# A transformer trunk's opening on one core: natural x tiles, two chunks transposed on TensorE, eight column tiles, modulation by VectorE row sums

## The chip, the cores and the metric

The kernel runs on one core of a Trainium2 chip. Its time is the device time of one launch in microseconds. A profile of one execution gives, for each engine (TensorE = PE, with its weight loads as PEld; VectorE = DVE; ScalarE = ACT; GpSimd = POOL; SyncE = SP, which issues most DMAs), every instruction with its start and its duration.

## The reference

Two inputs ("batches" 0 and 1), each 512 rows of 1024 columns, go through one layer with shared weights. What matters here is its beginning:

```python
def rms_norm(x, g):
    y = x * lax.rsqrt(jnp.mean(x * x, axis=-1, keepdims=True) + EPS)
    return y * g

c_act = jax.nn.silu(c)
mod = c_act @ w_ada + b_ada                       # (1024) @ (1024, 6*1024)
sh1, sc1, g1, sh2, sc2, g2 = split(mod, 6)
h = rms_norm(x, norm1_g) * (1.0 + sc1) + sh1
proj = h @ w_in                                   # (512, 1024) @ (1024, 2816)
q_a, k_a, v_a, q_r, k_r, v_r, g_r = split(proj, IN_OFFSETS, axis=-1)
...
x = x + g1 * (mix @ w_out)                        # mix: windowed attention and retention
h = rms_norm(x, norm2_g) * (1.0 + sc2) + sh2
x = x + g2 * (jnp.square(jax.nn.relu(h @ w_mlp1)) @ w_mlp2)
return rms_norm(x, final_g)
```

All is float32. A product is made of three matmuls of split operands: a high part (rounded to a shorter format, `fp32r`) and a low part (the rest); high × high, high × low, low × high.

## The kernel before

The work is staged in this order: an opening (batch 0's first norm, modulation and the first column tiles of its input projection), the mixer (the other projections of both batches, attention, retention, output projection), then the MLP for both batches together, and the last norm. Everything works on h transposed: 128 of the 1024 features on the partitions (a *chunk*, `kc` = 0 to 7), the 512 rows along the free axis.

The **opening** is written out by hand as a list of step names, `FRONT`; each name calls `step_<kind>(numbers)`, and the list's order is the order of each engine's instructions and of SP's DMA queue. Up to `P.7.0` this order is pinned. The steps that matter:

- `x.t` loads x. Before, this is a pair of chunks of x transposed on the host (`x0_t`, tile `xt`); `sq`, `ad` square them on ScalarE and add them on VectorE, `ns` sums over the partitions with a matmul against ones, `nc` and `nt` turn the sum into a column per row tile, `nv` adds epsilon, `nr` takes the power −0.5 on GpSimd.
- `rbt`, `rbc`: the factor of each row is spread over the partitions by four TensorE transposes (`row_factors`, tile `rb`) and copied; `xn`, `xh` multiply x by it on VectorE.
- `tr.kc.s` loads 128 columns of the modulation weights, transposed (s = 1 scale, 0 shift); `C.kc.s` multiplies them by the activated c, which `cbt`/`cbc` spread over all partitions (`cb`), and sums each row, one VectorE instruction of 1024 elements. Chunk 1 alone (`BOTH`) is summed for both batches by TensorE instead: `nat` loads, `pm` multiplies, `mr`, `pt`, `md` bring the result into columns.
- `wi.kc` loads the first `FIRST` columns of `w_in` for one chunk; `wh`, `wl` make their high and low parts.
- `hh`, `hm`, `hl` make the high part, the whole and the low part of h for one chunk from x, scale and shift.
- `P.kc.c`, `R.kc.c`, `Q.kc.c` are the three matmuls of chunk kc and column tile c into bank `first_c`. Eight PSUM banks exist.
- `warm.i.n` are n matmuls of zeros; `di`, `bias` make attention's distance table; `keep` stores the low parts for batch 1, and `rvl`, `rvh`, `rvs` start the next weights.

The **mixer** runs as *units* (`run_units`): one 128-column tile of a projection, with its weight load, split and 24 matmuls. Between halves of a unit, `between` looks up a digit in each of two strings: `SUMS` says how many background row sums (`background_mods`, one VectorE instruction of 1024 elements each, for all other modulation values) are issued there, `STAGES` how many steps of attention and retention. The first projection columns of batch 0 come out of the opening (`first`), all others are units. For batch 1 the high parts are made anew and the low parts are loaded back.

Of the kernel before, what the change touches and what calls it, by code (L numbers as in the profile page):

```python
# [15 lines left out]
P = 128  # L16
# [12 lines left out]
FIRST = 896  # L29
BOTH = (1,)  # L30
# [3 lines left out]
def trunk_kernel(ctx, tc, x0, x1, x0_t, x1_t, params, gate2_bias, w_ada_first, w_ada_t, w_ada_gate2, w_in_first, w_in,  # L34
# [143 lines left out]
    xt0 = {}  # L178
# [27 lines left out]
    gm = const.tile([P, NB, KC], F32, name="gm")  # L206

    def background_mods():


        todo = [(s, kc, (1,)) for kc in range(KC) if kc not in BOTH for s in (1, 0)]
# [6 lines left out]
        for n, (sec, kc, bs) in enumerate(todo):  # L218
            t, nxt = nxt, load(n + 1)
# [346 lines left out]
    def tick_stage(force=False):  # L566
# [4 lines left out]
        for a in active:  # L571
            if a[1] <= clock[0] or force:
# [60 lines left out]

    unit_of = {c: i for i, c in enumerate([*range(FIRST, 1792, P), *range(2304, 2816, P)])}

    def proj_unit(hT, col, name, done):
        key = f"in{col}"

        def load():
            if hT is hT_of[1]:  # L640
# [95 lines left out]
    def out_units(b, late=None):  # L736
# [46 lines left out]
        def unit(hf, kq):  # L783
# [4 lines left out]
            def load():  # L788
# [6 lines left out]
                if kq == 2:  # L795
                    gr[hf] = gate_row(0, b, hs)
# [207 lines left out]
    wi, raws, halves, sums, mr, hm, banks, open_banks = {}, {}, {}, {}, {}, {}, {}, {}  # L1004
    order = (4, 5, 0, 1, 2, 3, 6)
    kept_first = tc.dram_tile((P, KC, FIRST), F32, name="kept_first")
    for c in range(FIRST // P):
        kept_lows[f"in{c * P}"] = kept_first[:, :, c * P:(c + 1) * P]
# [52 lines left out]
    def step_ns(n):

        if n == 0:
            banks["ns"] = aux_bank("ns")
        src = one["sq", 0][:, 0, :] if n == 2 else one["sq", 3][:, n, :]
        nc.tensor.matmul(banks["ns"][:2, :], ones, src, start=n == 0, stop=n == 2)

    def step_nc():
        one["ns"] = f2("ns")
        nc.scalar.copy(one["ns"][:2, :], banks["ns"][:2, :])  # L1070

    def step_nt():
        for t in range(NT):
            nc.tensor.transpose(banks["ns"][:, 2 * t:2 * t + 2], one["ns"][:2, t * P:(t + 1) * P], ident[:2, :2])

    def step_nv():
        one["v"] = small([P, NT], "nv")
        nc.vector.tensor_scalar(one["v"], banks["ns"][:, 0:2 * NT].rearrange("p (t o) -> p t o", o=2)[:, :, 0], 1.0 / D, EPS,
                                ALU.mult, ALU.add)

    def step_nr():
        one["r"] = small([P, NT], "nr")
        nc.gpsimd.tensor_tensor(one["r"], one["v"], neghalf[:, :NT], ALU.pow)
# [11 lines left out]
    def step_xh(k):  # L1095
        nc.vector.tensor_tensor(xt0[0][:, k, :], xt0[0][:, k, :], banks["rb"], ALU.mult)

    def step_pm(kc, q):

        if q == 0:  # L1100
            sums[kc] = aux_bank(f"pm_{kc}")
        w = halves[kc, q // 2].rearrange("p (k n) -> p k n", n=256)
        for k in range(2 * q, 2 * q + 2):
            nc.tensor.matmul(sums[kc][:NB, :256], cact[:, k, :], w[:, k % 4, :], start=k == 0, stop=k == KC - 1,
                             skip_group_check=True)

    def step_mr(kc):
        mr[kc] = mwork.tile([NB, 256], F32, tag="st", name=f"mr_{kc}", bufs=8)
        nc.scalar.copy(mr[kc], sums[kc][:NB, :256])

    def step_pt(kc):
        for c in range(2):
            nc.tensor.transpose(sums[kc][:, 256 + c * 2:258 + c * 2], mr[kc][:, c * P:(c + 1) * P], ident[:NB, :NB])

    def step_md(kc):
        m = [sums[kc][:, 256 + c * 2:258 + c * 2] for c in range(2)]
        nc.vector.tensor_scalar(mod_a[0][:, kc, :], m[1], onep[:, kc:kc + 1], gcol[0][:, kc:kc + 1], ALU.add, ALU.mult)
        nc.vector.tensor_scalar(mod_s[0][:, kc, :], m[0], bcol[:, kc:kc + 1], None, ALU.add)
# [9 lines left out]
    def step_wh(kc):  # L1128
        w = [r4(f"wi{s}_{kc}").rearrange("p a n -> p (a n)")[:, :FIRST] for s in "hl"]
        nc.scalar.copy(w[0], wi[kc][:, :FIRST])  # L1130
        raws[kc], wi[kc] = wi[kc], w

    def step_wl(kc):
        w = wi[kc]
        nc.vector.tensor_sub(w[1], raws.pop(kc)[:, :FIRST], f(w[0]))
# [12 lines left out]
    def step_P(kc, c):  # L1148
        if kc == 0:
            open_banks[c] = (mm_bank if c < 3 else aux_bank)(f"first_{c}")  # L1150
        w, h_, cs = wi[kc], hm[kc][0], slice(order[c] * P, (order[c] + 1) * P)
        nc.tensor.matmul(open_banks[c], w[0][:, cs], h_[:, 0, :], start=kc == 0, stop=False)

    def step_R(kc, c):
        w, h_, cs = wi[kc], hm[kc][0], slice(order[c] * P, (order[c] + 1) * P)
        nc.tensor.matmul(open_banks[c], w[1][:, cs], h_[:, 0, :], start=False, stop=False)
# [23 lines left out]
    def step_rvs(kq):  # L1180
# [4 lines left out]
    steps = dict(rvl=step_rvl, rvh=step_rvh, rvs=step_rvs, x=step_x, nat=step_nat, tr=step_tr, wi=step_wi, tanh=step_tanh, cact=step_cact, cbt=step_cbt, cbc=step_cbc,  # L1185
                 sq=step_sq, ad=step_ad, ns=step_ns, nv=step_nv, nr=step_nr, rbt=step_rbt, rbc=step_rbc, xn=step_xn,
                 pm=step_pm, mr=step_mr, pt=step_pt, nc=step_nc, nt=step_nt, md=step_md, C=step_C, wh=step_wh, wl=step_wl, hm=step_hm, hh=step_hh,
                 hl=step_hl, P=step_P, R=step_R, Q=step_Q, xh=step_xh, keep=step_keep, warm=step_warm, di=masked_distance,
                 bias=bias_table)
    FRONT = """  # L1190
x.0 warm.0.11 x.1 x.2 di.0 di.1 x.3 di.2 bias.0 bias.1 tr.0.1 bias.2 bias.3 tanh sq.0 cact tr.0.0
cbt.0 bias.4 cbt.1 cbc.0 sq.1 warm.1.7 nat.1.0 bias.5 ad.1 sq.2 wi.0 cbt.2 cbt.3 cbc.1 sq.3.0
warm.2.2 ad.2 sq.3.1 ns.0 nat.1.1 bias.6 bias.7 ns.1 ad.3 wi.1 C.0.1 ns.2 warm.3.3 tr.2.1 nc cbc.2
nt pm.1.0 tr.2.0 nv cbc.3 nr wh.0 C.0.0 warm.4.2 wi.2 rbt pm.1.1 xh.0 pm.1.2 tr.3.1 wl.0 hh.0 hm.0
P.0.0 P.0.1 tr.3.0 P.0.2 rbc P.0.3 hl.0 P.0.4 P.0.5 xh.1 P.0.6 pm.1.3 wi.3 C.2.1 R.0.0 mr.1 R.0.1
wh.1 R.0.2 tr.4.1 R.0.3 pt.1 R.0.4 md.1 R.0.5 wl.1 R.0.6 hh.1 Q.0.0 tr.4.0 Q.0.1 Q.0.2 hm.1 Q.0.3
xn.1 Q.0.4 Q.0.5 wh.2 Q.0.6 wi.4 P.1.0 P.1.1 hl.1 P.1.2 P.1.3 C.2.0 P.1.4 P.1.5 tr.5.1 P.1.6 R.1.0
R.1.1 wh.3 R.1.2 C.3.1 R.1.3 R.1.4 tr.5.0 hh.2 R.1.5 R.1.6 Q.1.0 hm.2 Q.1.1 C.3.0 Q.1.2 Q.1.3 Q.1.4
Q.1.5 Q.1.6 P.2.0 wl.2 wi.5 P.2.1 hh.3 P.2.2 tr.6.1 P.2.3 P.2.4 hm.3 hl.2 P.2.5 P.2.6 R.2.0 wh.4
xn.2 R.2.1 tr.6.0 R.2.2 R.2.3 R.2.4 R.2.5 C.4.1 R.2.6 Q.2.0 Q.2.1 Q.2.2 Q.2.3 Q.2.4 C.4.0 Q.2.5  # L1200
Q.2.6 P.3.0 P.3.1 wh.5 P.3.2 P.3.3 wl.3 wi.6 tr.7.1 P.3.4 P.3.5 tr.7.0 hh.4 P.3.6 hl.3 hm.4 R.3.0
R.3.1 R.3.2 C.5.1 R.3.3 R.3.4 R.3.5 R.3.6 Q.3.0 Q.3.1 C.5.0 Q.3.2 Q.3.3 wh.6 Q.3.4 Q.3.5 Q.3.6 P.4.0
# [445 lines left out]
```

## Time and profile before

| What | Value |
|---|---|
| median of 3 runs | 1091.72 us (1091.71 to 1092.14) |
| the profiled execution | 1093.01 us, of which the span of its instructions is 1091.2 us |
| TensorE / VectorE / ScalarE / GpSimd busy in the span | 99% / 79% / 49% / 4% |
| mean DMA rate over the span | 204 GB/s |
| opening, to the last matmul into `first` | 58.3 us |

A row of the timeline reads: start, duration, engine, line, operation, output tile, inputs, shapes, count; in brackets how long the engine was idle before it, and what ended that. A duration includes the engine's start-up, which overlaps the instruction before, so what one instruction costs in a full stream is the distance from start to start. A row of waits reads: who waited for whom, us in total, times, longest.

### The profile page before, as it was taken

The numbers are of one execution on the slowest core, as the hardware profiler recorded it, in microseconds if no ns is written. First come the engines' busy times: TensorE is split into PE (matmuls) and PEld (weight loads), VectorE is DVE, ScalarE is ACT, GpSimd is POOL, SyncE is SP. The second block draws the span as 40 slices with busy tenths as digits, with TensorE's granted clock in tenths as the row PEclk, the third lists the DMA queues.
The fourth block names the chain that finished last, engine by engine and source line by source line (L and its number), as shares of the span: only waits on it lengthen the run. The fifth ranks groups of instructions, "written<-read, shape, count | busy, mean of one in ns | idle before, by whom it ended". The sixth has DMA issues, their size and how long they took to land.

```text
span 1091.2 us, 14043 instructions
## 1 busy us (share of the span) xinstructions
PE 1077.9 (99%) x5018; PEld 886.1 (81%) x5018; DVE 866.8 (79%) x1456; ACT 536.9 (49%) x907; POOL 48.6 (4%) x55
## 2 busy tenths in 40 slices
PE   9999999999999999999999999999999999999997
PEld 4878887778888888898788888888888888888886
DVE  7979988887878885999787787866569754589786
ACT  6477768547754442574333333433353633334342
POOL 0000000000000001010000000000000000003213
PEclk9999999999999999999999999999999999999999
DMA  9776877665556889535554455543973556525504
GB/s 368 262 265 208 285 267 250 209 226 177 186 178 209 290 305 355 178 115 191 180 173 169 145 193 174 184 145 108 327 298 114 180 192 215 186 78 193 193 20 155
DMA packets 85083, 222.24 MB, mean 204 GB/s; under 512 B 8195, under 2 KB 22547, under 8 KB 85013
## 3 DMA queue, kind: packets, MB, share of 16 engines
q1 hardware_dynamic: 84420, 220.76, 58.5%
q8 instruction: 39, 0.64, 0.2%
q10 hardware_dynamic: 432, 0.57, 0.2%
q14 instruction: 32, 0.25, 0.1%
q0 software_dynamic: 160, 0.02, 0.0%
HBM read 161.80 MB, written 59.52 MB: 203 GB/s over the span
## 4 chain that ended last, share of the span: by engine, by line
PE 51%; DVE 0%; POOLq 0%; issue 0%; ACT 0%; POOL 0%; ACTq 0%
PE x L1418 16%; PE px_None L967 13%; PE y L1418 12%; PE py_None L967 10%; PE pg L266 0%; PE pg L265 0%; DVE x2r L1487 0%; POOLq L1644 0%; DVE x2r L1460 0%; DVE acc L1459 0%; ACT jkf L1466 0%; POOL msf L1469 0%; ACTq L1466 0%
## 5 line engine op out<-in xcount | busy, mean ns | idle before, releaser
L1358 DVE TENSOR_TENSOR uc_l<-ur,uc_h 128x1024 fp32r<-128x1024 f32 x56 | 68.3, 1221 | 52.3 <-ACT uc_h L1358 35.1
L1418 PE MATMUL x<-wc_l,uc_h 128*128 128x512 f32 (+1 forms) x264 | 101.0, 383 | 0.0
L1418 PE MATMUL x<-wc_h,uc_l 128*128 128x512 f32 (+1 forms) x264 | 101.0, 383 | 0.0
L1418 PE MATMUL x<-wc_h,uc_h 128*128 128x512 f32 (+1 forms) x264 | 100.8, 383 | 0.0
L1358 ACT CAST uc_h<-ur 128x1024 fp32r<-128x1024 f32 x56 | 58.8, 1050 | 77.2 <-PE x L1418 25.1
L1418 PE MATMUL y<-wc_h,uc_h 128*128 128x512 f32 x192 | 74.7, 389 | 0.0
L1418 PE MATMUL y<-wc_l,uc_h 128*128 128x512 f32 x192 | 74.7, 389 | 0.0
L1418 PE MATMUL y<-wc_h,uc_l 128*128 128x512 f32 x192 | 74.7, 389 | 0.0
L1358 ACT CAST wc_h<-w 128x1024 fp32r<-128x1024 f32 x48 | 50.5, 1051 | 48.1 <-PE x L1418 24.7
L1358 DVE TENSOR_TENSOR wc_l<-w,wc_h 128x1024 fp32r<-128x1024 f32 x48 | 58.5, 1220 | 17.6 <-ACT wc_h L1358 13.8
L1418 PEld LDWEIGHTS x<-wc_h,uc_l 128*128 128x128 f32 x264 | 49.6, 188 | 9.7
L1418 PEld LDWEIGHTS x<-wc_h,uc_h 128*128 128x128 f32 x264 | 49.6, 188 | 9.7
L1418 PEld LDWEIGHTS x<-wc_l,uc_h 128*128 128x128 f32 x264 | 49.6, 188 | 9.6
L152 PE MATMUL po<-wh_wo,ms 128*128 128x512 f32 x128 | 50.4, 394 | 0.0
L153 PE MATMUL po<-wh_wo,ms 128*128 128x512 f32 x128 | 50.0, 390 | 0.0
L199 DVE CUSTOM_DVE_ANT_0 jka_b<-raw_adat,cb,cols 128x1024 bf16<-128x1024 f32 x39 | 49.0, 1280 | 0.1
L872 ACT CAST wc_s4h<-raw_w 128x1024 fp32r<-128x1024 f32 x16 | 16.9, 1054 | 63.7 <-PE px_None L967 49.5
L1418 PEld LDWEIGHTS y<-wc_h,uc_l 128*128 128x128 f32 x192 | 36.0, 188 | 7.5
L1418 PEld LDWEIGHTS y<-wc_h,uc_h 128*128 128x128 f32 x192 | 36.0, 188 | 7.4
L1418 PEld LDWEIGHTS y<-wc_l,uc_h 128*128 128x128 f32 x192 | 36.0, 188 | 7.4
L391 ACT ACTIVATE st<-st,negm 128x256 f32<-128x256 f32 (+1 forms) x64 | 35.2, 555 | 9.5 <-DVE negm L386 9.5
L967 PE MATMUL py_None<-hch,wc_a 128*128 128x512 f32 x120 | 39.6, 389 | 0.0
(393 smaller groups left out, 2957.6 us busy)
## 6 DMA issues: line engine op xcount, KB each, us to landing
ur<-spill SPq DMA_DIRECT2D x56, 512.0 KB, 4.5
raw_adat<-in_w_ada_t_dram SPq DMA_DIRECT2D x38, 512.0 KB, 5.4
raw_w<-in_w_mlp_dram SPq DMA_DIRECT2D x32, 512.0 KB, 3.6
spill<-s SPq DMA_DIRECT2D x64, 256.0 KB, 3.6
w<-in_w_mlp_dram SPq DMA_DIRECT2D x32, 512.0 KB, 4.7
spill<-u SPq DMA_DIRECT2D x48, 256.0 KB, 2.0
raw_ada<-in_w_ada_t_dram SPq DMA_DIRECT2D x14, 512.0 KB, 9.8
x<-in_x_dram SPq DMA_DIRECT2D x12, 512.0 KB, 7.3
```

The source lines that it names most:

```text
L152: nc.tensor.matmul(ps, lhs[0], rhs[0], start=start and not low_first, stop=False)
L153: nc.tensor.matmul(ps, lhs[late], rhs[1 - late], start=False, stop=stop and low_first)
L199: nc.vector.tensor_tensor_reduce(junk(f"jka_{name}_{sec}_{kc}_{b}"), t, cb[:, b, :], 1.0, bcol[:, sec * KC + kc:sec * KC + kc + 1] if bias ...
L391: nc.scalar.activation(st[hh][:, :w], st[hh][:, :w], AF.Exp, bias=negm[:, hh:hh + 1], scale=0.125, accum_out=den[:, hh:hh + 1])
L872: nc.scalar.copy(hi, src)
L967: self.last = nc.tensor.matmul(bank[:, cs], x[:, k, :], y, start=first and k == 0 and i == 0, stop=last and k == 3 and i == 2, skip_group_ ...
L1358: last_split[:] = [nc.scalar.copy(hi, src), nc.vector.tensor_sub(lo, src, f(hi))]
L1418: nc.tensor.matmul(out, left[n][x][:, i, ts_], right[n][y][:, i, cs], start=first and i == 0 and k == 0, stop=end and i == 1 and k == 2, s ...
```

## The change

The opening loads x for the norm in natural layout (128 rows of 1024), squares and sums each tile in one ScalarE instruction, and makes the factor per tile on GpSimd. The first 256 columns of x are scaled per row and transposed by TensorE, which gives chunks 0 and 1; chunks 2 to 7 still come from host-transposed pairs (`xp`). Chunk 1's modulation is made by row sums as all others, chunk 0's by halves of 512 (`Ch`), loaded in halves (`trh`). The opening makes eight column tiles instead of seven (the first retention key tile is the new one), and the projection columns are gathered on the host in the order in which they are used. Two guards, `made_through`, see to it that a background value is made before its reader is written. `SUMS`, `STAGES` and `FRONT` are new; of these a line each is shown.

```diff
-FIRST = 896
-BOTH = (1,)
+FIRST = (512, 640, 0, 128, 256, 384, 768, 1280)
+UNITS = tuple(c for c in (*range(768, 1792, P), *range(2304, 2816, P)) if c not in FIRST)
...
-        todo = [(s, kc, (1,)) for kc in range(KC) if kc not in BOTH for s in (1, 0)]
+        todo = [(s, kc, (1,)) for kc in range(KC) for s in (1, 0)]
...
-    SUMS = ("100100012110011201001001100022000002222100210020110002021021"
+    SUMS = ("110100021002200210100011000010021201221010002110100202120001"
...
+                    made_through(2, KC - 1)
                     gr[hf] = gate_row(0, b, hs)
...
     def step_x(t):
-        xt0[t] = load_x_pair(0, t)
+        xn0[t] = load_x_tile(0, t)
+
+    def step_xp(t):
+        xt0[t] = load_x_pair(0, t)
...
-    def step_nat(kc, kh):
-        t = halves[kc, kh] = r4f(f"raw_ada1_{kc}_{kh}")
-        in_order(nc.sync.dma_start(t, w_ada_first[BOTH.index(kc), kh]))
+    def step_trh(s, hf):
+        if hf == 0:
+            halves[0, s] = r4f(f"raw_ada1_0_{s}")
+        cs = slice(hf * 512, (hf + 1) * 512)
+        in_order(nc.sync.dma_start(halves[0, s][:, cs], w_ada_t[s, 0][:, cs]))
...
-    def step_sq(t, kc=None):
-        if not kc:
-            one["sq", t] = r4(f"sq_{t}", F32)
-        part = slice(0, 2) if kc is None else slice(kc, kc + 1)
-        nc.scalar.activation(one["sq", t][:, part, :], xt0[t][:, part, :], AF.Square)
-    def step_ad(t): ...
-    def step_ns(n): ...
-    def step_nc(): ...
-    def step_nt(): ...
+    def step_sq(t):
+        one["ss", t] = small([P, 1], f"ss_{t}")
+        nc.scalar.activation(junk(f"jkx_{t}"), xn0[t], AF.Square, scale=D ** -0.5, accum_out=one["ss", t])
+
+    def step_nv(t):
+        one["v", t] = small([P, 1], f"nv_{t}")
+        nc.gpsimd.tensor_scalar(one["v", t], one["ss", t], EPS, None, ALU.add)
+
+    def step_nr(t):
+        if t == 0:
+            one["r"] = small([P, NT], "nr")
+        nc.gpsimd.tensor_tensor(one["r"][:, t:t + 1], one["v", t], neghalf[:, 0:1], ALU.pow)
+
+    def step_xs(t):
+        part, r = xn0[t][:, :2 * P], one["r"][:, t:t + 1]
+        if t > 1:
+            nc.scalar.activation(part, part, AF.Copy, scale=r)
+        else:
+            nc.vector.tensor_scalar(part, part, r, None, ALU.mult)
...
+    def step_xt(t):
+        for c in range(2):
+            if t == 0:
+                banks["x", c] = (aux_bank, mm_bank)[c](f"pxc_{c}")
+            nc.tensor.transpose(banks["x", c][:, t * P:(t + 1) * P], xn0[t][:, c * P:(c + 1) * P], ident)
+
+    def step_xc():
+        one["x1"] = f2("xc1")
+        nc.scalar.copy(one["x1"], banks["x", 1])
+
+    def x_chunk(kc):
+        return banks["x", 0] if kc == 0 else one["x1"] if kc == 1 else xt0[kc // 2][:, kc % 2, :]
...
-    def step_pm(kc, q): ...
-    def step_mr(kc): ...
-    def step_pt(kc): ...
-    def step_md(kc): ...
+    def step_Ch(s, hf):
+        cs, a_ = slice(hf * 512, (hf + 1) * 512), (mod_s, mod_a)[s][0][:, 0, 0:1]
+        if hf == 0:
+            one["C", s] = small([P, 1], f"cs_{s}")
+        nc.vector.tensor_tensor_reduce(junk(f"jka_h_{s}_{hf}")[:, :512], halves[0, s][:, cs], cb[:, 0, cs], 1.0,
+                                       one["C", s] if hf else onep[:, 0:1] if s else bcol[:, 0:1], ALU.mult, ALU.add,
+                                       a_ if hf else one["C", s])
+        if hf and s:
+            nc.vector.tensor_tensor(a_, a_, gcol[0][:, 0:1], ALU.mult)
...
-    def step_wh(kc):
-        w = [r4(f"wi{s}_{kc}").rearrange("p a n -> p (a n)")[:, :FIRST] for s in "hl"]
-        nc.scalar.copy(w[0], wi[kc][:, :FIRST])
-        raws[kc], wi[kc] = wi[kc], w
+    def step_wh(kc, hf=None):
+        if not hf:
+            raws[kc], wi[kc] = wi[kc], [r4(f"wi{s}_{kc}").rearrange("p a n -> p (a n)") for s in "hl"]
+        cs = slice(0, 1024) if hf is None else slice(hf * 512, (hf + 1) * 512)
+        (nc.scalar.copy if hf is None else nc.vector.tensor_copy)(wi[kc][0][:, cs], raws[kc][:, cs])
...
     FRONT = """
...
+Ch.1.1 wi.1 nr.3 xt.2 warm.4.3 xs.3 Ch.0.0 xt.3 xp.1 rbt Ch.0.1 xc warm.5.5 wh.0.0 tr.2.1 hh.0
...
-    first = attn_units(hT_of[0], 0) + head_0[:1]
+    first = attn_units(hT_of[0], 0) + head_0[:2]
...
+    def made_through(sec, kc):
+        while background and made[-1:] in ([], [(sec, kc)]) or (sec, kc) not in made:
+            tick_background()
...
+            made_through(0, kc)
             h_high(1, kc, src, dst)
...
-    run_units(units, 1.3, {5: lambda: extra.append(norm_x1())}, 0.6)
+    run_units(units, 1.3, {4: lambda: extra.append(norm_x1())}, 0.6)
```

More of the change, by code (lines that the diff above doesn't have):

```diff
@@ L218, in background_mods @@
         for n, (sec, kc, bs) in enumerate(todo):
+            made.append((sec, kc))
             t, nxt = nxt, load(n + 1)
@@ L632, in run_units @@
                 hooks[n]()
-    unit_of = {c: i for i, c in enumerate([*range(FIRST, 1792, P), *range(2304, 2816, P)])}
+    unit_of = {c: i for i, c in enumerate(UNITS)}
     def proj_unit(hT, col, name, done):
@@ L1001, in store @@
                 nc.sync.dma_start(spill[g][p, :, i, :], t)
[L1004 to L1008, printed above, removed]
+    wi, raws, halves, hm, banks, open_banks = {}, {}, {}, {}, {}, {}
+    kept_first = tc.dram_tile((P, KC, 1024), F32, name="kept_first")
+    for c, col in enumerate(FIRST):
+        kept_lows[f"in{col}"] = kept_first[:, :, c * P:(c + 1) * P]
     def step_x(t):
+        xn0[t] = load_x_tile(0, t)
+    def step_xp(t):
         xt0[t] = load_x_pair(0, t)
-    def step_nat(kc, kh):
-        t = halves[kc, kh] = r4f(f"raw_ada1_{kc}_{kh}")
-        in_order(nc.sync.dma_start(t, w_ada_first[BOTH.index(kc), kh]))
+    def step_trh(s, hf):
[3 more added lines that the diff above has]
+        in_order(nc.sync.dma_start(halves[0, s][:, cs], w_ada_t[s, 0][:, cs]))
     def step_tr(kc, s):
@@ L1061, in step_ns @@
[L1061 to L1074, printed above, removed]
@@ L1093, in step_xn @@
         x_scale(xt0[t], one["rb"])
[L1095 to L1118, printed above, removed]
+    def step_Ch(s, hf):
[7 more added lines that the diff above has]
+            nc.vector.tensor_tensor(a_, a_, gcol[0][:, 0:1], ALU.mult)
     def step_C(kc, s):
@@ L1183, in step_rvs @@
         first_v[kq].loaded([x.rearrange("p (a n) -> p a n", n=512) for x in w])
[L1185 to L1189, printed above, removed]
@@ L1190, in trunk_kernel @@
-    FRONT = """
[L1191 to L1195, printed above, removed]
@@ new lines, in trunk_kernel @@
+    FRONT = """
+x.0 x.1 warm.0.11 di.0 x.2 di.1 di.2 x.3 bias.0 trh.1.0 bias.1 bias.2 trh.1.1 bias.3 trh.0.0 tanh
+sq.0 cact trh.0.1 cbt.0 cbt.1 nv.0 cbc.0 sq.1 warm.1.4 wi.0 nr.0 cbc.1 cbt.2 xs.0 nv.1 sq.2 tr.1.1
+nr.1 cbt.3 cbc.2 warm.2.3 xs.1 nv.2 sq.3 cbc.3 xt.0 tr.1.0 nr.2 xt.1 warm.3.6 Ch.1.0 xs.2 nv.3
+Ch.1.1 wi.1 nr.3 xt.2 warm.4.3 xs.3 Ch.0.0 xt.3 xp.1 rbt Ch.0.1 xc warm.5.5 wh.0.0 tr.2.1 hh.0
+wh.0.1 hm.0 P.0.0 wl.0 P.0.1 tr.2.0 P.0.2 rbc P.0.3 P.0.4 bias.4 P.0.5 hl.0 P.0.6 bias.5 P.0.7 wi.2
@@ L1604, in _laid_out @@
                             + [np.tile(a[n].reshape(1, -1), (P, 1)) for n in ('ret_decay_fwd', 'ret_decay_bwd', 'attn_sink')], 1)
-    units = np.concatenate([w_in[:, FIRST:1792], w_in[:, 2304:2816]], 1)
+    columns = lambda cols_: np.concatenate([w_in[:, c:c + P] for c in cols_], 1)
     out = dict(
```

80 lines of the change are left out of this document (38 added, 42 removed).

## The prediction

> **What bounds the kernel now.** I read the page's busy shares first, then the span cut at the first projection matmul and at the end of the opening, then TensorE's waits and its timeline.
>
> ```profile
> PE 1077.9 (99%) x5018; PEld 886.1 (81%) x5018; DVE 866.8 (79%) x1456; ACT 536.9 (49%) x907; POOL 48.6 (4%) x55
> 0.00:17.66 17.66, 15.41 (x67) 6.20 (x67) 13.06 (x26) 11.29 (x19) 2.56 (x8) 1.00 0.91 347
> 17.66:58.30 40.64, 40.29 (x175) 31.82 (x175) 34.30 (x55) 21.91 (x31) 0.00 (x0) 1.00 0.82 310
> 58.30:250.00 191.70, 189.30 (x912) 154.71 (x911) 170.92 (x404) 130.43 (x261) 5.05 (x5) 1.00 0.70 239
> 17.66 1.66 PE L1152 MATMUL first<-h,wih 128*128 128x512 f32 x6
> 19.66 0.47 PE L1152 MATMUL first<-h,wih 128*128 128x512 f32 x1 [0.35 <-DVE xt L1096]
> 20.07 1.02 PE L1104 MATMUL pm<-raw_ada,cact 128*2 128x256 f32 x4
> 29.52 1.75 PE L1152 MATMUL first<-h,wih 128*128 128x512 f32 x7
> 31.11 1.75 PE L1156 MATMUL first<-h,wil 128*128 128x512 f32 x7
> 58.31 0.39 PE L152 MATMUL pj_rv<-wh_rv,h 128*128 128x512 f32 x1
> ```
>
> A row of stretches reads: length, then busy time of PE, PEld, DVE, ACT, POOL, granted clock, DMA share, GB/s. TensorE is busy 99% of the span, so outside the opening a saving is worth something only if it takes TensorE work away or lets that work begin earlier. In the first 17.66 us TensorE is busy too, but with `warm` matmuls and small sums: no product of the reference's projections is made before `P.0.0` at 17.66. From there it never stops for long, so the end of the kernel is, to first order, the start of `P.0.0` plus the TensorE work behind it plus the few waits. Seven matmuls go by in 31.11 − 29.52 = 1.59 us, 0.227 each; seven column tiles of three products and eight chunks are 168 of them, 38.1 us, while the opening takes 58.31 − 17.66 = 40.65. The 2.5 over are 0.35 of waiting, 1.0 for the four `pm` matmuls inside the stream, and some 1.1 of slow first matmuls, small transposes and slips.
>
> **The start of `P.0.0`.** In the old opening the last wait before it is a chain through the sum of squares, the transposed factor and the scaled x. In the new one the chain is: last x tile lands, ScalarE squares it with a row sum, GpSimd adds epsilon and takes the power, ScalarE scales 256 columns, TensorE transposes, then the rows of the factor and five `warm` matmuls that stand ahead of `P.0.0` on TensorE.
>
> On GpSimd, between the identity matrix and the first norm of batch 1, stood one power over four columns:
>
> ```order
> L487 IOTA dl 128x896
> masks.py:199 AFFINE_SELECT ident<-ident 128x128
> L1083 TENSOR_TENSOR nr<-nv,neghalf 128x4
> L1244 TENSOR_TENSOR r_x_1566<-v_x_1281,neghalf 128x4
> L470 TENSOR_TENSOR rrs_0_1904<-rva_0_1902,neghalf 128x4
> ```
>
> Now, at the same place (`nv` is the mean square plus epsilon, `nr` its power −0.5):
>
> ```order
> masks.py:199 AFFINE_SELECT ident<-ident 128x128
> L1062 TENSOR_SCALAR nv_160<-ss_142 128x1
> L1067 TENSOR_TENSOR nr<-nv_160,neghalf 128x1
> L1062 TENSOR_SCALAR nv_181<-ss_163 128x1
> L1067 TENSOR_TENSOR nr<-nv_181,neghalf 128x1
> L1062 TENSOR_SCALAR nv_199<-ss_183 128x1
> L1067 TENSOR_TENSOR nr<-nv_199,neghalf 128x1
> L1062 TENSOR_SCALAR nv_224<-ss_201 128x1
> L1067 TENSOR_TENSOR nr<-nv_224,neghalf 128x1
> ```
>
> Epsilon moved from VectorE to GpSimd, and four pairs in a row stand ahead of everything that x feeds. On ScalarE the squares and the first chunk stood so:
>
> ```order
> L1052 ACTIVATE sq_172<-xt_2_123 128x1024
> L1052 ACTIVATE sq_187<-xt_3_128 128x512 x2
> L505 ACTIVATE bias_t<-di 128x384 x2
> L1070 COPY ns<-ns 2x512
> L1130 CAST wih_229<-raw_wi_174 128x896
> L308 ACTIVATE h_0_0_251<-xt_0_105,mod_s_89,mod_a_87 128x512
> ```
>
> and now (`x` is a natural tile, `pxc`/`xc` the two transposed chunks):
>
> ```order
> L1058 ACTIVATE jkx_184,ss_183<-x_2_125 128x1024
> L1058 ACTIVATE jkx_202,ss_201<-x_3_129 128x1024
> L1072 ACTIVATE x_2_125<-x_2_125,nr 128x256
> L1072 ACTIVATE x_3_129<-x_3_129,nr 128x256
> L1084 COPY xc_252<-pxc_207 128x512
> L310 ACTIVATE h_0_0_264<-pxc_205,mod_s_89,mod_a_87 128x512
> ```
>
> The weight cast has left ScalarE's queue (VectorE does it), bias tables moved behind `h`, and two scalings that wait for GpSimd stand ahead of `h`.
>
> ```profile
> 0.73 1.83 SPq L175 DMA_DIRECT2D xt<-in_x_t_dram  x4
> DMA to landing us min/median/max: 4.5/6.1/6.9
> GB/s 0 116 357 419 423 415 407 406 410 406 414 401 413 412 407 412 409 393 419 126 8 271 393 325 76 367 382 244 256 0 19 197 358 409 421 429 397 419 390 416
> 14.03 0.94 ACT L1130 CAST wih<-raw_wi 128x896 fp32r<-128x896 f32 x1 [0.70 <-DMA raw_wi<-in_w_in_first_dram]
> L294 ACT ACTIVATE jk<-x 128x1024 bf16<-128x1024 f32 x4 | 4.2, 1062 | 0.0
> L399 ACT ACTIVATE st<-st,rden 128x256 f32<-128x256 f32 x8 | 3.6, 500 | 0.7 <-DVE rden L396 0.7
> 16.67 0.81 ACT L308 ACTIVATE h<-xt,mod_s,mod_a 128x512 fp32r<-128x512 f32 x1 [1.70 <-DVE xt L1096]
> 7.08 1.67 PE L1172 MATMUL warm<-idle 128*128 128x512 bf16 x7
> 15.26 0.65 PE L301 MATMUL rb<-ident,nr 128*128 128x128 f32 x4
> 1062.41 0.27 POOL L1469 TENSOR_SCALAR msf<-ssf,msf 128x1 f32<-128x1 f32 x1 [13.15 <-ACT jkf L1466]
> 1065.96 2.11 POOL L1473 TENSOR_TENSOR rf<-msf,neghalf 128x1 f32<-128x1 f32 x4
> 1043.92 0.80 POOL L1469 TENSOR_SCALAR msf<-ssf 128x1 f32<-128x1 f32 x1 [0.34 <-ACT jkf L1466]
> 1043.45 1.22 DVE L1358 TENSOR_TENSOR wc_l<-w,wc_h 128x1024 fp32r<-128x1024 f32 x1
> ```
>
> The first x tile lands at 0.73 + 4.5 = 5.2; behind it the queue moves some 410 GB/s, 1.28 us for 512 KB. (Check: old `wi.0` is six such loads and one of 448 KB later, 5.2 + 7.7 + 1.1 = 14.0, where the cast that waited for it starts.) So x.3 lands at 9.05. Its square takes 1.06 and about 0.1 for reading the sum: 10.25. GpSimd: 0.27 for epsilon and 0.54 for the power, 11.1. Beside it VectorE runs row sums with two SBUF operands; the 0.80 row, which ended 0.05 after the VectorE subtraction beside it, shows that such an operation can hold GpSimd. For this the bounds are 0 and one 512-wide row sum (half of 1.28) for each of the two, 1.3; I take 0.5, nearer to the lower end, since VectorE waits for the landing of a half between these row sums and lets go there: 11.65. Scaling 256 columns 0.50, two transposes 0.3 (quarters of the 0.65), rows of the factor 0.65, five `warm` (`warm.5.5` in the new table) at 0.24: 14.3; six hand-offs at about 0.05 make it **14.6** (13.9 without the GpSimd hold and with shorter hand-offs; 15.5 with both holds whole). The branch over `xc` (0.6) and `h` (0.81) is shorter, 14.0. The modulation is no later: four halves of 256 KB land by 9.05 + 2.56 = 11.6, and the last row sum ends near 13.3; `wi.0` lands at 12.9 and its first half is cast by 13.7.
>
> So `P.0.0` comes 17.66 − 14.6 = 3.1 us earlier.
>
> **The opening's length.** Eight columns are 192 matmuls, 43.6 us. The wait of 0.35 and the 1.0 of `pm` are gone, and its small transposes with it; of the slips I keep 1.0. VectorE has to keep pace:
>
> ```profile
> 36.36 1.28 DVE L199 CUSTOM_DVE_ANT_0 jka_f<-raw_ada,cb,onep 128x1024 bf16<-128x1024 f32 x1
> 37.76 1.28 DVE L199 CUSTOM_DVE_ANT_0 jka_f<-raw_ada,cb,cols 128x1024 bf16<-128x1024 f32 x1
> 38.97 1.08 DVE L1135 TENSOR_TENSOR wil<-raw_wi,wih 128x896 fp32r<-128x896 f32 x1
> 39.97 0.68 DVE L314 TENSOR_TENSOR h<-hm,h 128x512 fp32r<-128x512 f32 x1
> 40.57 1.22 DVE L305 TENSOR_TENSOR xt<-xt,rb 128x1024 f32<-128x1024 f32 x1
> ```
>
> By starts, a chunk costs it 1.40 + 1.21 for the two row sums, 1.00 × 1024/896 = 1.14 for the low halves, 0.60 for `hl` and half of 1.14 for `xn`: 4.9 us against 24 × 0.227 = 5.45 on TensorE. Chunk 1, formerly summed on TensorE, now costs VectorE 2.6 here: after `hl.0` (about 16.0) its two sums end near 18.7, `h` of chunk 1 near 19.5, due at 14.6 + 5.45 = 20.05. It fits by half a microsecond and the slack grows by 0.5 a chunk. The loads grow from 27 to 31 times 512 KB (x a second time for three pairs, weights of 512 instead of 448 KB); at 1.28 each the last could land at 43.6, wanted near 47. Hidden, with 3 us to spare. ScalarE was busy 21.9 of 40.6 and takes four bias rows more; hidden. End: 14.6 + 43.6 + 1.0 = 59.2, 0.9 later than before, with one column tile more done.
>
> **Behind the opening.** One projection unit is gone: 24 × 0.227 = 5.45 us of TensorE. Against this VectorE gets two more 1024-wide row sums in the background (chunk 1 of batch 1) and loses one weight split, and has 5.45 us less time for the rest.
>
> ```profile
> L199 DVE CUSTOM_DVE_ANT_0 jka_b<-raw_adat,cb,cols 128x1024 bf16<-128x1024 f32 x39 | 49.0, 1280 | 0.1
> L102 DVE TENSOR_TENSOR wl_rk<-raw_rk,wh_rk 128x1024 fp32r<-128x1024 f32 x4 | 4.9, 1220 | 0.0
> PE psc L381 <- DVE mx L383: 0.6, 1, 0.6
> PE pj_rq L148 <- DVE wl_rq L102: 0.5, 1, 0.5
> PE pyb L480 <- ACT ryn L475: 0.4, 1, 0.4
> PE pj_rv L152 <- DVE qs L359: 0.3, 1, 0.3
> PE pvt_a L344 <- ACT vt_a L338: 0.3, 1, 0.3
> PE pj_rv L152 <- DVE ks L332: 0.2, 1, 0.2
> ```
>
> From 58.3 to 250 VectorE is idle 191.70 − 170.92 = 20.8 us and TensorE waits 2.3 in all (the six rows). With +2.6 − 1.2 of work and 5.45 less time the idle is 13.9; in proportion the waits become 2.3 × 20.8/13.9 = 3.4. I take +1.0. The bounds are −1 (new tables that leave half of today's waits) and +4 (VectorE's extra work plus half of the lost 5.45 shows). `made_through` issues no wait of its own; it can only bunch row sums, which this bound covers. The hook moved from unit 5 to 4 is the same unit. Longer `keep` stores and one more strided load lie under a DMA share of 0.70.
>
> **Sum.** +0.9 − 5.45 + 1.0 = −3.55 against the profiled execution's 1093.01 gives 1089.5; that execution is 1.3 above the runs' median, so against 1091.72 the forecast is **1088.2**, a gain of 0.33%. Alone its range is 1085.9 (start at 13.9, waits of −1 and fewer slips) to 1089.5.
>
> **Rivals.** First, GpSimd's first `TENSOR_SCALAR`.
>
> ```profile
> 1000.59 12.82 POOL L1469 TENSOR_SCALAR msf<-ssf 128x1 f32<-128x1 f32 x1 [238.74 <-ACT jkf L1466]
> 1011.01 2.35 DVE L1460 TENSOR_TENSOR x2r<-x2r,acc 128x1024 f32<-128x1024 f32 x2
> 1013.61 1.23 DVE L1358 TENSOR_TENSOR wc_l<-t,wc_h 128x1024 fp32r<-128x1024 f32 x1 [0.25 <-ACT wc_h L1358]
> 14.17 1.04 POOL L1083 TENSOR_TENSOR nr<-nv,neghalf 128x4 f32<-128x4 f32 x1 [12.07 <-DVE nv L1078]
> ```
>
> The first one of the program took 12.82 us where later ones take 0.27. If it is the price of a first use, the new opening pays it in the chain: `nv.0` is ready at 5.2 + 0.3 + 1.15 = 6.7 and ends at 19.5; its power and three more pairs (3.0 and hand-offs) end at 22.8, and the 3.0 from there to `P.0.0` make 25.8, 11.2 later; VectorE is then ahead, half a microsecond comes back: **1099**. It decides from a first use of 5.2 us (delay F − 1.65 against the gain of 3.55). For it speaks that it was the first; against it that it ended 0.05 us after the first gap that VectorE left (1013.36), and that the power's own first use, at 14.17, cost nothing and GpSimd's other kinds in the opening neither. The Trainium skill (GPSIMD Engine Reference, section 2.1 Instruction dispatch) gives about 6 us for the first call of a freshly loaded kernel; no row of this trace shows a 6; by that alone the delay would be an estimated 4.35 and the time 1092.5. The Trainium skill (SBUF — State Buffer, Who interferes with whom) has a VectorE instruction with two SBUF inputs hold a GpSimd one that reads SBUF for one whole instruction; the 0.80 row agrees, and by it a hold is counted above as 0 to 1.3.
>
> Second, VectorE gives the gain back: 95% busy in places behind the opening, it is late by 2 to 5 us in sum. The six waits are its sort already; against it, none is over 0.6. Time 1089.6 to 1093, taken as 1091.
>
> Third, a first use of some 5 to 7 us, by the delay F − 1.65 a time of 1091.5 to 1093.5.
>
> **Chances.** A run tells a kernel apart from no change by about 0.2%, 2.2 us. Forecast 0.66; VectorE gives it back 0.12 (0.02 of it slower); first use of 12.8 us 0.17; a middling one 0.05 (no change). Faster 0.66, same 0.15, slower 0.19. To 1092.5 the range holds the first two and part of the third, about eight in ten.
>
> **What would show it.** The first `first<-h,wih` matmul at 13.9 to 15.5; `nv` on GpSimd at 0.2 to 0.8; no wait over 0.5 before chunk 1; the first `pj_rv` matmul near 59.2; TensorE's waits from there to 460 near 3.3 us. An `nv` row of 5 us or more, `P.0.0` beyond 18, or a sum of waits over 6 would make it wrong.

## The result: 1085.76 us, and where the 6 us came from

| | before | after |
|---|---|---|
| median (4 runs each) | 1091.85 us | 1085.76 us (1085.64 to 1086.17) |
| ratio | | 0.9945, 95% interval 0.9927 to 0.9962 |
| profiled execution, and its span | 1093.01, 1091.2 | 1085.64, 1083.9 |

The change gains 6.1 us where 3.55 were forecast, and 1085.76 lies 0.14 below the range. Unaltered in a later set of runs the changed kernel took 1086.31 beside 1092.18 for before, ratio 0.9947 (0.9933 to 0.9962).

The span up to the first projection matmul, and from there to the end of the opening (length, busy time of PE, PEld, DVE, ACT, POOL, granted clock, DMA share, GB/s):

```profile
0.00:14.19 14.19, 11.72 (x61) 6.43 (x61) 10.25 (x29) 9.64 (x19) 5.90 (x15) 1.00 0.90 339
14.19:57.84 43.65, 43.65 (x193) 36.16 (x193) 38.53 (x59) 25.27 (x35) 0.00 (x0) 1.00 1.02 408
```

The second row says the most: 43.65 us of stage, 43.65 busy. 192 matmuls at the 0.227 of a full stream are 43.6, so there is no wait and no slip in it at all. The stage ends at 57.84, 0.47 earlier than before, with one column tile more done. TensorE's timeline at both ends, and the steps that lead to the first product (PEld is the weight load of the matmul):

```profile
9.88 0.78 POOL L1062 TENSOR_SCALAR nv<-ss 128x1 f32<-128x1 f32 x1 [0.33 <-ACT jkx L1058]
10.74 1.06 POOL L1067 TENSOR_TENSOR nr<-nv,neghalf 128x1 f32<-128x1 f32 x1
11.83 0.51 ACT L1072 ACTIVATE x<-x,nr 128x256 f32<-128x256 f32 x1 [1.64 <-POOL nr L1067]
12.39 0.44 PE L1080 MATMUL pxc<-ident,x 128*128 128x128 f32 x2 [0.39 <-ACT x L1072]
12.67 0.60 PE L303 MATMUL rb<-ident,nr 128*128 128x128 f32 x4
13.10 1.24 PE L1162 MATMUL warm<-idle 128*128 128x512 bf16 x5
13.35 0.79 ACT L310 ACTIVATE h<-pxc,mod_s,mod_a 128x512 fp32r<-128x512 f32 x1
14.19 1.68 PEld L1142 LDWEIGHTS first<-h,wih 128*128 128x128 f32 x8 [0.34 <-ACT h L310]
14.19 2.11 PE L1142 MATMUL first<-h,wih 128*128 128x512 f32 x8
...
57.84 0.39 PE L152 MATMUL pj_rv<-wh_rv,h 128*128 128x512 f32 x1
```

Behind the opening TensorE waits no more than before, 2.1 in place of 2.3 from 58 to 460 us (who waited for whom, us in total, times, longest):

```profile
PE pyn L463 <- ACT ryt L459: 1.2, 2, 0.8
PE pj_rv L152 <- DVE qs L361: 0.5, 1, 0.5
PE ppt L409 <- ACT st L401: 0.2, 1, 0.2
PE pyb L482 <- ACT ryn L477: 0.2, 1, 0.2
```

Laid over each other matmul by matmul, the two executions stand 0.47 apart at the end of the opening and 5.86 at 410 us: that, and one unit of 5.45 less in between. Near 524 us before's profiled execution loses another 1.2 that after's does not, one TensorE wait of 0.8 and its hand-overs in the MLP. That is about the 1.3 by which before's profile lay above its median, so it is not counted as gain.

So three terms of the forecast are off, by some 2.5 us together: the start of the first product (14.19 and not 14.6), the slips of the opening (0 and not 1.0) and the mixer (not +1.0 but −0.2 by its waits, +0.1 by the matmuls laid over each other). The experiments take them in the order of what they turned out to weigh.

### The profile page after: what moved, and what is told of

Read it like the earlier page. It is cut to its first block, busy times and chain, and to the rows that moved or that the text cites. A ratio compares the mean times of both kernels' runs of the same rounds, so it can differ in the third digit from the quotient of the medians.

```text
span 1083.9 us, 14046 instructions
## 1 busy us (share of the span) xinstructions
PE 1071.9 (99%) x5005; PEld 886.1 (82%) x5005; DVE 868.2 (80%) x1465; ACT 535.8 (49%) x909; POOL 53.1 (5%) x62
## 4 chain that ended last, share of the span: by engine, by line
PE 87%; DVE 6%; ACT 3%; issue 1%; DMA 1%; POOL 1%; SPq 0%; POOLq 0%; ACTq 0%; DVEq 0%
PE x L1415 16%; PE px_None L971 15%; PE y L1415 12%; PE py_None L971 11%; PE po L152 3%; PE po L153 3%; PE po L148 3%; DVE jka_b L199 2%; PE psc L383 2%; PE po L416 2%; PE ppt L409 2%; PE first L1142 1%; PE first L1150 1%; PE first L1146 1%; PE pj_rv L148 1%; PE pj_rv L152 1%
## 5 line engine op out<-in xcount | busy, mean ns | idle before, releaser
L1355 DVE TENSOR_TENSOR wc_l<-w,wc_h 128x1024 fp32r<-128x1024 f32 x48 | 58.5, 1219 | 17.6 <-ACT wc_h L1355 13.6
## 6 DMA issues: line engine op xcount, KB each, us to landing
raw_ada<-in_w_ada_t_dram SPq DMA_DIRECT2D x14, 512.0 KB, 10.2
```

Source lines behind the costliest of these rows:

```text
L1355: last_split[:] = [nc.scalar.copy(hi, src), nc.vector.tensor_sub(lo, src, f(hi))]
```

## Experiments

### The tables alone

```diff
-    SUMS = ("110100021002200210100011..."      # the changed kernel's
-    STAGES = ("220212301252323112420411..."
+    SUMS = ("100100012110011201001001..."      # before's
+    STAGES = ("110503214210121121122112..."
```

> The changed kernel with the two tables of before (where the background row sums and the stages of attention and retention are issued between projection units). Theory 'the tables pay': the extra work on VectorE and the shorter mixer do cost what the prediction called +1.0, and the new tables take it back; with the old ones, which count one unit more, TensorE's waits from 58 to 460 us rise from 2.1 to 4-8 and the time is 1087.5-1091. Rival 'VectorE had room': the term was never there, whatever the tables; waits 1.8-3, time 1085.3-1086.5. The opening (first product 14.2, first pj_rv 57.8) is the same in both.

Measured: 1104.53 us, ratio to before 1.0113 (1.0099 to 1.0127). That is 18 us above the changed kernel and 12 above before. The opening is the same (first product 14.28, first `pj_rv` 57.93); all of the loss is behind it, 18.1 us by 430. Its waits of TensorE from 58 to 460 are 13 us:

```profile
PE pyb L482 <- ACT ryn L477: 3.1, 5, 1.0
PE pvt_a L346 <- ACT vt_a L340: 2.6, 1, 2.6
PE pj_k L153 <- DVE h L316: 1.7, 2, 1.3
PE po L152 <- ACT ms L782: 1.3, 1, 1.3
PE psc L383 <- ACT pt L320: 1.0, 1, 1.0
...
```

"The tables pay" holds in kind, but both the 13 us of waits and the time lie far outside what it gave (4 to 8 us, at most 1091). How one such wait is made can be read in the timeline of that run around 212 us:

```profile
203.09 1.28 DVE L199 CUSTOM_DVE_ANT_0 jka_b<-raw_adat,cb,cols 128x1024 bf16<-128x1024 f32 x1
...
204.30 1.28 DVE L199 CUSTOM_DVE_ANT_0 jka_b<-raw_adat,cb,cols 128x1024 bf16<-128x1024 f32 x1
...
205.62 0.69 DVE L439 SCALAR_TENSOR_TENSOR rsf<-prs,dtab 128x512 f32<-128x512 f32 x1
...
209.65 0.16 DVE L475 SCALAR_TENSOR_TENSOR rnb<-mv,rrs 128x4 f32<-128x4 f32 x1 [1.18 <-POOL rrs L472]
209.91 1.50 ACT L477 ACTIVATE ryn<-pyn,rnb,rrs 128x128 f32<-128x128 f32 x4 [2.94 <-DVE rnb L475]
211.29 0.59 ACT L340 COPY vt_a<-pj_v 128x512 f32<-128x512 f32 x1
211.94 0.66 PE L346 MATMUL pvt_a<-ident,vt_a 128*128 128x128 f32 x4 [2.57 <-ACT vt_a L340]
```

Two row sums stand on VectorE ahead of the steps of a score (`rsf`) and of the statistics of a norm. The norm's factors (`rnb`) come at 209.65; ScalarE, in order, waits 2.94 for them with `ryn`, and `vt_a`, a copy whose input is done since 195 us, stands behind it. TensorE waits for the copy. In the next two runs the same wait is 0.9 with the new sums and the old stages, and under 0.15 with the old sums and the new stages, so it takes both old tables to make the 2.57. No engine is overloaded: VectorE is busy 333 of these 402 us, less than the 349 of the changed kernel.

### Which of the two tables

One edit each: `SUMS` new with `STAGES` old, and the reverse.

> The changed kernel with its own table of row sums and before's table of stages. Theory 'sums': the damage of the old tables (18.8 us) comes from row sums on VectorE ahead of a norm; with the sums right it falls to 1086-1091. Rival 'stages': two stages of attention or retention issued too close leave too few matmuls between their dependent steps; 1096-1106 even with the sums right.

> The changed kernel with before's table of row sums (two sums short of what the eight-column opening leaves over) and its own table of stages. Theory 'sums': most of the 18.8 us is here, 1096-1106, with waits for h of batch 1 and for ryn behind pairs of row sums. Rival 'stages': 1086-1091.

Measured: 1099.45 us (ratio to before 1.0065, 1.0048 to 1.0082) with the old stages, 1094.86 (1.0027, 1.0016 to 1.0038) with the old sums; the unaltered changed kernel beside them 1086.31.

> The changed kernel unaltered, beside these runs. Every theory: 1085.4-1086.6, within 0.1% of the first measurement.

Old stages cost 13.1, old sums 8.6, both 18. Neither theory had it whole; stages weigh more. The waits tell only a part of the second: of its 8.6, some 2.5 are waits of TensorE from 58 to 460, 4.6 in place of 2.1. The largest waits of the first run, then the largest of the second:

```profile
PE po L416 <- ACT pt L320: 3.0, 2, 2.8
PE pyb L482 <- ACT ryn L477: 2.5, 4, 0.8
```

```profile
PE pyn L463 <- ACT ryt L459: 2.2, 2, 1.7
```

With the old stages, `po`, a step of attention, finds its input not yet copied; with the old sums, a retention step does. That the steps stand too close is the reading of the rows; no run moved a single step.

### Old tables put in step by hand

```diff
-    SUMS = "1001000121" "100112..."            # before's; the unit taken out had digits 9 and 10
-    STAGES = "1105032142" "101211..."
+    SUMS = "11010021" "111112..."              # the rest as before
+    STAGES = "22151332" "101211..."
```

> The changed kernel with the tables of before, put in step with its units by hand: the two digits of the unit that is gone are taken out (their ticks go to the digits beside), and two row sums more are issued in the first fourteen digits, so that from there on each unit has the sums and stages behind it that it had before. Theory 'step': the 18.8 us of the old tables came from their being out of step (two sums late, stages one unit early); in step the waits of TensorE from 58 to 460 fall from 13 to 2-5 and the time to 1086-1089. Rival 'content': the shorter mixer needs another distribution; above 1092.

Measured: 1108.49 us, ratio 1.0148 (1.0134 to 1.0162): worse than the tables out of step. The "step" theory falls in this form. In step (the stages from the ninth digit on, the sums from the fourteenth), but with 19 stages squeezed into the first eight digits, the kernel has one wait of 4.7 us that the other tables don't have:

```profile
95.33 2.90 PE L409 MATMUL ppt<-ident,st 128*128 128x128 f32 x12 [4.71 <-ACT st L401]
```

There the transposes of one block of attention are issued right behind the product of another (`po`, done near 90.6), with no projection matmuls in between to cover the softmax that they read. The other large losses (behind 180 us) stayed, so being in step was not their whole cure either.

### Seven columns in the new opening

`FIRST` without 1280, weights of 896 columns, `P`, `R`, `Q` of the eighth column gone, one unit more behind, before's tables.

> The changed kernel's opening with seven column tiles as before (weights of 896 columns, one more projection unit later, the tables of before). Theory 'the eighth column is neutral': 24 matmuls cost 0.227 each in either place, the opening runs 168 matmuls in 38.2 without a wait, first pj_rv at 14.2+38.2=52.4, and the time stays at 1085.3-1086.5. Rival 'VectorE is late with seven columns': TensorE takes 4.77 us a chunk and VectorE 4.9, so TensorE waits 0.3-1 us in several chunks, first pj_rv at 53.4-55, time 1086.8-1088.5; the eighth column is then what gives VectorE its room.

Measured: 1102.04 us, ratio 1.0091 (1.0078 to 1.0105). The time was far outside both expectations. The excess is behind the opening, where before's tables now meet two row sums more (chunk 1 of batch 1). What the run was for stands in its opening, ahead of all tables; the stage as one stretch, and the worst place of its timeline, with what stands ahead of it:

```profile
14.36:54.52 40.16, 39.12 (x169) 31.30 (x169) 36.74 (x57) 23.30 (x33) 0.00 (x0) 1.00 1.03 401
```

```profile
42.66 0.08 DVE L199 DVE_READ_ACCUMULATOR2_ANT mod_s<- 128x1 f32 x1
43.12 0.94 ACT L1121 CAST wih<-raw_wi 128x896 fp32r<-128x896 f32 x1 [2.68 <-DMA raw_wi<-in_w_in_first_dram]
43.97 0.81 ACT L310 ACTIVATE h<-xt,mod_s,mod_a 128x512 fp32r<-128x512 f32 x1
44.83 1.90 PE L1142 MATMUL first<-h,wih 128*128 128x512 f32 x7 [0.89 <-ACT h L310]
```

168 matmuls need 38.2; the stage took 40.16. The rival had the size right (53.4 to 55 for the first `pj_rv`, here 54.52), and its cause in part. With seven columns a chunk gives VectorE 4.77 us and it wants 4.9; for chunk 2 `h` waits for the row sums, and TensorE 0.15 for `h`. But the worst wait, 0.89, is made by a load: the row sums of chunk 6 are done at 42.74, while on ScalarE the cast of the last weights, which stands ahead of `h`, waits for their landing until 43.12. The DMA share of the stage is 1.03. The eighth column is not neutral. It is worth 2.0 us here, because it covers both VectorE and the loads; how the 2.0 divide between them was not measured.

```diff
-    SUMS = ("1001000121...
+    SUMS = ("1101100121...                     # two sums more in the first five digits
```

> The seven-column kernel of above with one edit: two row sums more in its first five digits of the table, so that every later sum is as far as in the kernel before. Theory 'step': its 13 us behind the opening came from being two sums behind; the waits fall to 2-4 and the time to 1087.3-1089 (the changed kernel plus the 2.1 that its opening loses with seven columns). Rival 'load': VectorE has two sums too many wherever they are put; 1092 or more.

Measured: 1095.79 us, ratio 1.0034 (1.0022 to 1.0047). Two row sums moved to the front of one string took 6.2 us of some 14 away and left about 7.5. The time lies where the rival put it (1092 or more), but the rival held that the place of the two sums does not matter, and it was worth 6.2. So "step" has a part of it, and neither theory the whole.

### Before, with row sums for chunk 1

`BOTH = ()`: `nat`, `pm`, `mr`, `pt`, `md` replaced by two loads and two row sums; before's tables.

> The kernel before, with chunk 1's modulation by VectorE row sums as for the other chunks, in place of the four TensorE sums, the copy, the two transposes and the two VectorE steps. First product stays near 17.7. Theory 'the sums on TensorE are the slips': chunk 0 of before takes 7.1 us in place of 4.77 because of them and what switches around them; without them 17.7 to first pj_rv falls from 40.65 to 38.8-39.7 and the time to 1089.8-1091. Rival 'VectorE is late instead': the two row sums (2.6) push h of chunk 1 behind the end of chunk 0 at 22.4, TensorE waits 0.5-2 there; 40.2-41.5 and 1091.3-1092.8.

Measured: 1105.01 us, ratio 1.0118 (1.0104 to 1.0132); the opening from first product to first `pj_rv`, and TensorE's waits (the 1.6 is the one ahead of the first product, outside the stage):

```profile
17.32:58.65 41.33, 39.58 (x169) 31.25 (x170) 36.57 (x59) 21.70 (x30) 0.00 (x0) 1.00 0.81 303
```

```profile
PE first L1155 <- ACT h L311: 2.2, 3, 1.6
PE first L1159 <- DVE wil L1138: 1.2, 2, 0.9
```

41.33 is within the rival's bounds and 0.7 longer than before's 40.65; 1.8 of it are waits, 0.6 for `h` and 1.2 for the low halves of the weights, both behind VectorE. Taking the TensorE sums out of seven columns gains nothing, since VectorE's row sums cost as much again; it takes the eighth column to hide them. The time is outside both expectations, since behind the opening some 12.5 us are lost: before's tables cost their price a third time.

### The start alone

`warm.5.5` became `warm.5.20`.

> The changed kernel with 20 in place of 5 warm matmuls ahead of the first product, which comes 15 x 0.238 = 3.6 us later at most (3.3-3.6: near 17.6). Theory 'the start sets the end': the whole delay is seen, 1089.0-1089.5. Rival 'a later limit absorbs it': VectorE and the loads get ahead and waits in the mixer go, so under two thirds of it is seen, 1085.8-1088.2.

Measured: 1089.71 us, ratio 0.9978 (0.9969 to 0.9987). Against the changed kernel's 0.9945 that is 3.6 us of loss.

```profile
17.36 2.21 PE L1142 MATMUL first<-h,wih 128*128 128x512 f32 x8
...
61.11 0.39 PE L152 MATMUL pj_rv<-wh_rv,h 128*128 128x512 f32 x1
```

Both stand 3.2 to 3.3 later, and the shift is still 3.27 at 460 us. The start sets the end, one to one; nothing absorbs it. (The profiled execution has 0.7 more from the MLP, behind 500 us, where before's had its 1.2.)

### What holds GpSimd in the opening

```diff
-        nc.vector.tensor_tensor_reduce(..., halves[0, s][:, cs], cb[:, 0, cs], 1.0,
+        nc.vector.tensor_tensor_reduce(..., banks["cb", hf], halves[0, s][:, cs], 1.0,
```

> The changed kernel with one operand of the four opening row sums read from the PSUM banks of c instead of its copy in SBUF; nothing else. Theory 'two SBUF operands hold GpSimd': nv and nr of the last x tile fall from 0.78 and 1.06 to about 0.25 and 0.57, the last scaling comes at 10.8-11.0 instead of 11.83; the first product moves little, since the sums still end near 13 and the copy of the second chunk still stands ahead of h: 13.9-14.2, time 1085.2-1086.2. Rival 'the hold has another cause': 0.78 and 1.06 as before.

Measured: 1086.60 us, ratio 0.9949 (0.9937 to 0.9962), no difference to the changed kernel. The last `nv` and `nr`, and what leads to the first product:

```profile
10.47 0.22 POOL L1062 TENSOR_SCALAR nv<-ss 128x1 f32<-128x1 f32 x1 [0.41 <-ACT jkx L1058]
10.78 0.57 POOL L1067 TENSOR_TENSOR nr<-nv,neghalf 128x1 f32<-128x1 f32 x1
13.49 0.78 ACT L310 ACTIVATE h<-pxc,mod_s,mod_a 128x512 fp32r<-128x512 f32 x1 [0.32 <-DVE mod_s L1103]
14.32 2.12 PE L1142 MATMUL first<-h,wih 128*128 128x512 f32 x8 [0.26 <-ACT h L310]
```

The hold is real and is that of two SBUF operands: 0.22 and 0.57 in place of 0.78 and 1.06 (0.22 and 1.14 in the later profile of the unaltered changed kernel). (The first x landed 0.3 later in this execution, so all times are later by that.) The hold wasn't what set the start: the row shows `h` waiting for the last row sum.

### The long first instruction in the tail

Four `TENSOR_SCALAR` of one column more on GpSimd, behind the stores of `gates`.

> The changed kernel with a TENSOR_SCALAR of 128x1 on GpSimd more behind each of the four stores of gates near 619, 639, 734 and 754 us; its result isn't used. Theory 'VectorE's chain': the 12.83 us of the tail's first one is time in which VectorE's instructions overlap without a gap; the new ones take 0.25 to a few us, each until VectorE's next gap, and the tail's first keeps 10-14. Rival 'price of return after hundreds of us': the first of the new ones takes 12-13 wherever VectorE stands, and the tail's first falls to 0.2-1.

Measured in one run: 1086.44 us. The first of the new ones, the tail's first, and VectorE's rows where it ends:

```profile
620.95 0.38 POOL L272 TENSOR_SCALAR dummy<-adacc 128x1 f32<-128x1 f32 x1
994.30 12.83 POOL L1468 TENSOR_SCALAR msf<-ssf 128x1 f32<-128x1 f32 x1 [238.20 <-ACT jkf L1465]
1004.73 2.35 DVE L1459 TENSOR_TENSOR x2r<-x2r,acc 128x1024 f32<-128x1024 f32 x2
1007.35 1.22 DVE L1357 TENSOR_TENSOR wc_l<-t,wc_h 128x1024 fp32r<-128x1024 f32 x1 [0.26 <-ACT wc_h L1357]
```

After 600 us without one, the new one takes 0.38, and the tail's first keeps its 12.83. That ends at 1007.13, just behind VectorE's first gap, which opens at 1007.09. So the 12.83 of the prediction's first rival was never the price of a first use, nor of a return after hundreds of us. That it is a wait for VectorE to pause is inferred from where it ends, 0.05 behind that gap here and in before; no run moved the gap.

### A shorter start

Row sums from PSUM as above, the two copies of batch 1's c moved to ScalarE, `hh.0` ahead of `xc`, fewer `warm`, `P.0.7` behind `R.0.1`.

> The changed kernel with its start shortened: row sums as in the run with PSUM operands, the two copies of batch 1's c on ScalarE, h of chunk 0 ahead of the copy of chunk 1, three warm matmuls in place of five at the last place (two fewer elsewhere), the eighth column's first product two places later. Theory: the sums end near 12.1, wi.0 lands at 12.6 and its first half is cast by 13.0: first product 13.0-13.4, first pj_rv 56.7-57.1, time 1084.5-1085.2. Rival: chunk 0 or 1 gives it back (a bank or h late), or the mixer's table is out of step with it; first pj_rv 57.3 or later, 1085.5-1086.5.

Measured: 1087.06 us, ratio 0.9955 (0.9941 to 0.9969): better than before, not better than the changed kernel.

```profile
9.71 0.75 DVE L1103 CUSTOM_DVE_ANT_0 jka_h<-pcb,raw_ada,onep 128x512 bf16<-128x512 f32 x1 [0.86 <-DMA raw_ada<-in_w_ada_t_dram]
13.94 1.90 PE L1142 MATMUL first<-h,wih 128*128 128x512 f32 x7 [0.80 <-ACT h L310]
```

VectorE, free 0.9 us sooner, waits for the first half of the modulation weights until 9.71, so the row sums start only 0.13 earlier, and the first product comes at 13.94 and not 13.0 to 13.4. The time is 0.6 above the rival's upper end. By 150 us the 0.25 has turned into a lag of 0.5 behind the changed kernel, by 370 into one of 0.9, with no single wait there over 0.8. What takes it was not settled; the tables were made for the other start.

## Why the prediction was wrong in size

**The start** (14.6; 14.19). The prediction had the wrong path end last. It took TensorE's own queue, and put the branch over `xc` and `h` at 14.0, shorter. In the profiled execution the weight load waits 0.34 for `h`, which ends at 14.14. In the later profile of the unaltered changed kernel it is plainer:

```profile
13.42 0.78 ACT L310 ACTIVATE h<-pxc,mod_s,mod_a 128x512 fp32r<-128x512 f32 x1 [0.32 <-DVE mod_s L1103]
14.25 2.11 PE L1142 MATMUL first<-h,wih 128*128 128x512 f32 x8 [0.26 <-ACT h L310]
```

There GpSimd's last `nr` ended at 11.26, against 11.80 in the first (11.65 was reckoned), and the first product came no sooner. The prediction followed the modulation to its last row sum (13.3; measured 13.1 and 13.4), but did not add the 0.8 of `h` behind it. TensorE's queue was mis-sized as well: I added up durations, 0.3, 0.65 and 1.2, of instructions that run in a stream; from start to start the rows give 0.28, 0.43 and, by the twenty `warm` of the delayed kernel, 1.04. So it was free near 14.1, close to `h` by chance. The prediction used that rule for VectorE and not here. The start then carries over one to one, as the delayed kernel shows.

**The slips of the opening** (1.0; 0). This term contradicted the prediction's own working: VectorE had been worked out at 4.9 us a chunk against 5.45 on TensorE, so nothing was left to slip. Before's excess of 2.5 us, its TensorE sums among it, is of the size that seven columns had in either other form: 2.0 in the new opening, 3.1 in the old one with row sums. The chunk-1 step had it right that the sums fit by half a microsecond: h of chunk 1 was ready at 19.2, chunk 0 ended at 19.8. The loads were said to be hidden with 3 us to spare; the last landed at 44.13 in place of 43.6, and since its cast stands on ScalarE ahead of `h` of chunk 6, which was ready at 45.92 and wanted at 46.96, the room was 1.0.

**The mixer** (+1.0; −0.2). This is the step that failed in kind. The prediction took VectorE's mean idle time, scaled six waits by it, and let "new tables" stand for a bound of −1. Idle time on average says nothing here. With the same work on every engine and other tables the kernel takes 1094.9, 1099.5, 1104.5 and 1108.5 us, so the tables decide over a range of 22 us, more than three times the whole gain, and over the sign. The bound of +4 would have been broken by every other table that was run. That the new ones fit was not to be seen in anything the prediction had weighed; the term came near zero through them alone, so it is luck that the forecast of +1.0 lies as near as it does.

**The rivals.** A long first use on GpSimd did not come: the opening's first `nv` took 0.24. The prediction had the reason in hand, the gap of VectorE at which the tail's row ended, and gave it 0.17 all the same. "VectorE gives it back" did not happen in the changed kernel. The four others do give it back, with 9 to 22 us in place of 2 to 5, but not because VectorE has too much to do: it is less busy there than in the changed kernel, and part of their waits are for steps of attention.

**A lost microsecond costs more than one.** With the old tables TensorE idles 11.3 us more from 58 to 460 than in the changed kernel, and loses 18. The rest is slow matmuls: 402 − 13.6 us of busy time for 1841 of them, 0.211 each, against 0.208, which is 5.7 us. A part of that is the clock. Behind the wait of 2.57, which ended at 211.94, that run shows (the column ahead of the last two is the granted clock)

```profile
212.70:216.00 3.30, 3.30 (x11) 2.67 (x10) 2.27 (x4) 1.24 (x3) 0.00 (x0) 0.50 0.52 159
216.10:220.00 3.90, 3.90 (x19) 3.23 (x18) 2.62 (x5) 2.21 (x4) 0.00 (x0) 1.00 0.02 4
```

Some 3.4 us at half clock are 1.7 us of work; where the other 4 come from stays open. In before with row sums the clock fell in the last moments of a wait of 2.3, which ended at 207.45, and was still at half through a second one of 1.7:

```profile
200.00:207.10 7.10, 5.13 (x25) 3.91 (x23) 5.85 (x18) 3.83 (x6) 1.01 (x1) 1.00 1.06 302
207.20:209.80 2.60, 2.35 (x7) 1.51 (x7) 0.58 (x2) 2.56 (x7) 0.00 (x0) 0.50 0.99 312
209.80:211.50 1.70, 0.05 (x1) 0.00 (x0) 1.67 (x3) 1.57 (x3) 0.00 (x0) 0.50 0.10 39
```

The Trainium skill (TensorE: Matmul & The Clock Gate, Part 1: The HAM clock gate) has the clock fall to half after an idle window of some 3.4 us. The 0.50 agrees; in these two runs no single wait was that long.

## What to carry to other kernels

Where an order of issue is planned, count it as part of the change: run the change with the old plan before believing a sum over work, since engines that issue in order turn a misplaced 1.3 us instruction into a wait on a third engine. Cover an engine or a load that is nearly late with more work per step on the one that waits (here an eighth column: 5.45 against 4.9), and then reckon its slips at nothing. In a stream, add starts and not durations, and follow each rival path to the instruction that needs it.

## What the hardware showed that was not expected

VectorE held GpSimd for 12.83 us, across a dozen instructions with two SBUF operands that follow without a gap, and the GpSimd instruction ended 0.05 behind the first gap. The Trainium skill (SBUF — State Buffer, Who interferes with whom) has such an instruction contend with a GpSimd one that reads SBUF; the run with one operand in PSUM agrees (0.22 and 0.57 in place of 0.78 and 1.06). That instructions following closely add up to one long hold is what the tail's row shows beyond it.

A single TensorE wait of 2.57 us in one run, and of 2.3 in another, went with a fall of the granted clock to 0.50, for 3.4 and 10.2 us (in the second case with another wait, of 1.7, within them), in mixers that otherwise stand at 1.00.
